# Both output projections as seven quadrant products, with weight sums formed in DRAM

## The chip, the cores and the metric

The kernel runs on one core of a Trainium2 chip. The metric is the device time of one execution in microseconds (us), lower is better; the median of several runs is compared. The core has a matrix engine (TensorE, PE in the profile, with its weight loads shown apart as PEld), a vector engine (DVE), a scalar engine (ACT), a general engine (GpSimd, POOL) and SyncE (SP), whose queue issues nearly all DMA transfers here. The engines run side by side, each through its own instructions in a fixed order, and wait for one another by semaphores. The program on each engine is fixed when the kernel is built.

## What is computed

A decoder trunk of two layers over 512 tokens of width 1024. Each layer normalises x, projects it with one matrix into the inputs of four head groups, mixes, gates, concatenates the four outputs to y (512 x 1024) and adds one output projection to the residual stream:

```python
def hybrid_layer(x, positions, ..., w_out):
    h = rmsnorm(x, norm_g)
    p = h @ w_in
    ...
    y = jnp.concatenate([o_a * jax.nn.silu(g_a), o_b * jax.nn.silu(g_b),
                         o_c * jax.nn.silu(g_c), o_d * jax.nn.silu(g_d)], axis=-1)
    return y @ w_out

for l in range(DEPTH):
    x = x + hybrid_layer(x, ...)
```

All of it is float32. The kernel keeps that precision on PE by splitting every operand into a high and a low part (type fp32r) and making three products of them: high x high, high x low, low x high.

## The kernel before

The 1024 rows of k are cut into eight tiles of 128 (`KT`), the tokens into four (`NT`). A "unit" is 512 KB of weights: `load_units` brings it from DRAM into one of two raw buffers (`rawS`), `split_units` makes its high part on ACT (or DVE) and its low part on DVE, in two halves, into one of six slots (`wS`). Loads and splits run ahead of their use as far as free buffers let them.

`Order` and `Chain` are a planner. Each piece of work is a generator which carries an estimated time (`ch.t`); the planner resumes the generators by due time and priority and so writes the instructions of each engine in the order in which it expects them to become ready. Nothing is reordered on the chip: an instruction whose operand is late holds up all that stand behind it on its engine, DMA issues on the queues of SP and POOL included.

A layer runs in this order on PE: `c` (low-rank inputs of the latent attention), the two token-major units `sq` and `kv`, sixteen feature units (`ga` to `gc1`), with the attention heads woven between them, and then the output projection, `o` in the profile. `put_y` splits a finished row block of y into `yTh` and `yTl` (`yD` for the last two). The last to be finished is block 5, after the last feature product `gc1`.

The output projection runs two column halves of 512, four token tiles each; each (half, token tile) is eight k tiles with three matmuls of 512 columns, accumulated in one PSUM bank (`part`, `YORDER`). `out_chain` adds the bank to the residual row tile `L.x[t]` on DVE; in layer 0 it also sums squares on ACT, sends the finished row tile to DRAM (`x1d`) and starts `pre_norm` of layer 1: two small POOL operations for the factor, a scaling `h` on DVE, eight transposes `hT` on PE, and a split into `hTh` and `hTl`, which `cq` of layer 1 reads. The last token tile of layer 1 is done in two pieces of 256 columns (`TAIL`), so that the end is short.

POOL also builds the rotary tables at the start and turns rotary pairs of Q and K (`rope`), which the attention heads wait for.

Of the kernel before, what the change touches and what calls it, by code (L numbers as in the profile page):

```python
# [196 lines left out]
def hybrid_trunk(ctx: ExitStack, tc: tile.TileContext, x, positions, norm_g, w_c, w_f, w_t, w_o, mla_q_norm_g,  # L197
# [52 lines left out]
    def mm3(ch, n, dst, sh, sl, mh, ml, first, last):  # L250
        c = cost(n)
        yield from ch.pe(c, PE.matmul, dst, sh, mh, start=first, stop=False)
        yield from ch.pe(c, PE.matmul, dst, sh, ml, start=False, stop=False)
        yield from ch.pe(c, PE.matmul, dst, sl, mh, start=False, stop=last)

    def dma(ch, nbytes, dst, src):

# [32 lines left out]
    def add_unit(*a):  # L290
        u = Unit(*a)
        units[u.name] = u
        u.idx = len(order)
        order.append(u)

    FEATS = ["ga0", "ga1", "ch0", "ch1", "cb0", "cb1", "cc0", "cc1", "gb0", "gb1", "su0", "su1",
             "gc0", "gc1", "gd0", "gd1"]
    TOKS = {"sq": ("sv", "mq"), "kv": ("mk", "mv")}
# [2 lines left out]
    for l in range(DEPTH):  # L301
        for kq in range(4):
            add_unit(w_c[l, kq], 2, 416, f"c{kq}_{l}")
        add_unit(mla_w_uq[l], 2, 384, f"uq_{l}")
        add_unit(mla_w_ukv[l], 1, 512, f"ukv_{l}")
        for n in SEQ:
            if n in TOKS:
                for kq in range(4):
                    add_unit(w_t[l, list(TOKS).index(n), kq], 2, 512, f"{n}{kq}_{l}")
            else:  # L310
                add_unit(w_f[l, FEATS.index(n)], 8, P, f"{n}_{l}")
        for half in range(2):
            for kq in WORDER:
                add_unit(w_o[l, half, kq], 2, 512, f"wo{half}{kq}_{l}")

    def load_units():
        for u in order:
            ch = Chain(o)
            u.raw_slots = rawS
            if u.name in ("c2_0", "c3_0"):  # L320
# [60 lines left out]
    hTh = big.tile([P, KT, S], F32R, name="hTh")  # L381
    hTl = big.tile([P, KT, S], F32R, name="hTl")
    yTh = big.tile([P, KT - 2, S], F32R, name="yTh")
    yTl = big.tile([P, KT - 2, S], F32R, name="yTl")

# [125 lines left out]
    for l in range(DEPTH):  # L511
        L = Layer()
        L.l = l
        L.ng_ev = Event()
        L.hT = [[Event(), Event()] for _ in range(NT)]
        L.xss = [cst.tile([P, 4], F32, name=f"xss{t}_{l}") for t in range(NT)]
        L.qd = [Event() for _ in range(NT)]
        L.kd = [Event() for _ in range(NT)]
        L.stat = [Event() for _ in range(NT)]
        L.Vt, L.Mt, L.gates, L.gate_ev, L.MD = {}, {}, {}, {}, {}  # L520
        L.md_ev = {n: [Event() for _ in range(NT)] for n in ("mq", "mk", "mv")}
        L.vt_ev = [Event() for _ in range(NT)]
# [4 lines left out]
        L.mix_ev, L.mla_ev, L.QK_ev = Event(), Event(), Event()  # L527
        L.x = [None] * NT
# [15 lines left out]
    def pre_norm(L, t, xx, t0, release):  # L544
        ch = Chain(o, t0)
        s1 = L.xss[t]
        yield from ch.pool(G.tensor_scalar, s1[:, 2:3], s1[:, 0:1], s1[:, 1:2], EPS, op0=ALU.add, op1=ALU.add)
        yield from pow_rstd(ch, s1[:, 3:4], s1[:, 2:3], 1)
        yield from ch.wait(L.ng_ev)
        h = yield from hS.get(ch, f"h{t}_{L.l}")  # L550
        hput = shared(hS, 2)
        tps = []
        for c in range(2):
            sl = slice(c * 512, (c + 1) * 512)
            yield from ch.dve(V.scalar_tensor_tensor, h[:, sl], in0=xx[:, sl], scalar=s1[:, 3:4], in1=L.ng[c],
                              op0=ALU.mult, op1=ALU.mult)
            tps.append(ch.t)
        release(ch)
        if t == NT - 1:
            for _ in range(2):  # L560
                (t2S if L.l else sS).put(ch)

        def half(c):
            c2 = Chain(o, tps[c])
            tp = yield from trS.get(c2, f"hT{t}_{c}_{L.l}")
            for k in range(4):
                kt = c * 4 + k
                yield from c2.pe(109.0, PE.transpose, tp[:, k * P:(k + 1) * P], h[:, kt * P:(kt + 1) * P], ident)
            hput(c2)
            yield from split2(c2, hTh[:, c * 4:c * 4 + 4, t * P:(t + 1) * P],  # L570
                              hTl[:, c * 4:c * 4 + 4, t * P:(t + 1) * P], tp.rearrange("p (k n) -> p k n", k=4))
            trS.put(c2)
            o.set(L.hT[t][c], c2.t)
        for c in range(2):
            o.spawn(half(c))

    def rope(ch, x1, x2, cb, sb, nh, nd, name):
        tab = yield from rbS.get(ch, f"rb{name}")
# [77 lines left out]
    def q_chain(L, t, q_ps, t0):  # L656
        ch = Chain(o, t0)
        l = L.l
        if t == 0:
# [121 lines left out]
    def y_tiles(L, kt):  # L781
        hi, lo = (yTh, yTl) if kt < 6 else L.yD
        return hi[:, kt % 6, :], lo[:, kt % 6, :]

    def put_y(ch, L, kt, yv):
        if kt == 6:
            L.yD = []
            for i in range(2):
                L.yD.append((yield from ydS.get(ch, f"yD{i}_{L.l}", [P, 2, S], F32R)))
        yield from split2(ch, *y_tiles(L, kt), yv)  # L790
        o.set(L.y[kt], ch.t)

    def su_chain(j):
        def f(L, a, t0):
# [237 lines left out]
    def mla_heads(L):  # L1032
# [37 lines left out]

        yield from heads(L, "a", L.Vt, prep, qk)
        o.set(L.mla_ev, o.now)

    def moba_heads(L):
        ch0 = Chain(o)
# [69 lines left out]
    def out_chain(L, half, t, a, t0, c0=0, c1=512):  # L1145
# [10 lines left out]
        elif half == 1:  # L1156
# [5 lines left out]
                v4S.put(c2)  # L1162
            o.spawn(pre_norm(layers[l + 1], t, L.x[t], ch.t, release))


    def main():
        m = Chain(o)

        def tok(L, n, width, t, dst, us):

            for k in range(KT):
                if n == "c" and k % 4 == 0:
                    yield from m.wait(L.hT[t][k // 4])
                if t == 0 and k % 2 == 0:
                    us.append((yield from unit(m, f"{n}{k // 2}_{L.l}")))
                wh, wlo = us[k // 2]
                yield from mm3(m, width, dst, hTh[:, k, t * P:(t + 1) * P], hTl[:, k, t * P:(t + 1) * P],
                               wh[:, k % 2, :], wlo[:, k % 2, :], k == 0, k == KT - 1)
                if t == NT - 1 and k % 2 == 1:
                    done_unit(f"{n}{k // 2}_{L.l}")  # L1180
                yield o.now

        def done_unit(name):
            if units[name].slots is not eS:
                units[name].slots.put(m)

        early_put(m)
        for L in layers:
# [19 lines left out]
            for n in SEQ:  # L1208
# [10 lines left out]
                else:  # L1219
                    a = yield from accS.get(m, f"{n}_{l}")  # L1220
                    wh, wlo = yield from unit(m, f"{n}_{l}")
                    for k in range(KT):
                        yield from mm3(m, S, a, wh[:, k, :], wlo[:, k, :], hTh[:, k, :], hTl[:, k, :],
                                       k == 0, k == KT - 1)
# [4 lines left out]
            for half in range(2):  # L1229
                us = {}  # L1230

                def part(t, a, i0, i1, c0=0, c1=512):
# [42 lines left out]
    def start():  # L1275
# [52 lines left out]
        hS.put(ch)  # L1328
        o.set(L0.ng_ev, ch.t)

    o.spawn(start())
    o.run()

# [49 lines left out]
```

## Time and profile before

| what | value |
|---|---|
| median of 3 runs | 509.28 us (508.9 to 509.54) |
| the profiled execution | 508.65 us, its span 506.8 us |
| DMA, all transfers | 51.57 MB, mean 102 GB/s |
| output projection, layer 0 / layer 1 | 214.4 to about 260.6 us / 459.5 to 503.4 us |

Times inside the profile count from the start of the span; what lies between the span and the execution's time is start and end of the program. A line of the groups view names the source line (nearly all are one helper's line, so tiles are the better name), engine, operation, written and read tiles, shapes and count, then the busy time, the mean of one, and the idle time of the engine just before these, with what ended it. In the timeline the columns are start, length, engine, line, operation; "x3" is three instructions run into one another; a time in brackets is idle time before. Lengths of neighbours overlap, since engines are pipelined: the step from one start to the next is what an instruction costs in a row of its kind.

### The profile page before, as it was taken

What the parts mean: (1) busy time and instruction counts of PE and PEld (TensorE: products, weight loads), DVE (VectorE), ACT (ScalarE), POOL (GpSimd) and SP (SyncE); (2) the same over time, 40 slices, a digit from 0 to 9 for tenths busy, and PEclk for the clock granted to TensorE, in tenths of its full rate; (3) what the DMA queues carried; (4) which work ended last, traced back from release to release, by engine and by line L of the source; (5) the groups of instructions that cost most, each with busy time, mean ns of one, the idle gap of its engine ahead of it and who ended that gap; (6) DMA issues with size and microseconds to landing.
All of it is one profiled execution on the core that took longest, in us unless ns stands there. A gap on an engine that the chain in (4) does not pass through costs nothing.

```text
span 506.8 us, 7665 instructions
## 1 busy us (share of the span) xinstructions
PE 498.1 (98%) x2508; PEld 423.3 (84%) x2508; DVE 349.3 (69%) x917; ACT 296.5 (58%) x891; POOL 139.2 (27%) x321
## 2 busy tenths in 40 slices
PE   6999999999999999999999999999999999999997
PEld 4898888888888888888889988888888888888886
DVE  4877975468799887635576988777868887635311
ACT  5698764567687775424247894677766777432100
POOL 6867875452000000000121488513330000000000
PEclk9999999999999999999999999999999999999999
DMA  8533415112114123464443242140142121624111
GB/s 273 165 123 114 125 43 166 41 43 66 60 43 166 52 74 109 142 175 117 143 155 126 83 125 71 55 124 2 42 167 82 43 83 49 201 84 164 66 54 50
DMA packets 20618, 51.57 MB, mean 102 GB/s; under 512 B 5985, under 2 KB 7265, under 8 KB 20578
## 3 DMA queue, kind: packets, MB, share of 16 engines
q1 hardware_dynamic: 20546, 51.08, 31.1%
q8 instruction: 20, 0.33, 0.3%
q0 software_dynamic: 32, 0.00, 0.1%
q14 instruction: 20, 0.16, 0.1%
HBM read 46.87 MB, written 4.19 MB: 101 GB/s over the span
## 4 chain that ended last, share of the span: by engine, by line
PE 90%; POOL 4%; DVE 2%; DMA 2%; ACT 1%; issue 1%; POOLq 0%; DVEq 0%
PE o L184 17%; PE kv L184 10%; PE cq L184 6%; PE sq L184 5%; PE cc L184 4%; PE gb L184 4%; PE cb L184 4%; PE gd L184 4%; PE gc L184 4%; PE ch L184 4%; PE su L184 4%; PE sa L184 3%; PE ga L184 3%; PE oa L184 2%; PE od L184 2%; PE sd L184 2%
## 5 line engine op out<-in xcount | busy, mean ns | idle before, releaser
L158 DVE TENSOR_TENSOR xr<-o,xr 128x512 f32<-128x512 f32 (+1 forms) x17 | 11.2, 658 | 42.0 <-PE o L184 42.0
L184 PE MATMUL o<-whi_wo,yTl 128*128 128x512 f32 (+1 forms) x102 | 38.4, 377 | 0.0
L184 PE MATMUL o<-wlo_wo,yTh 128*128 128x512 f32 (+1 forms) x102 | 38.4, 377 | 0.0
L184 PE MATMUL o<-whi_wo,yTh 128*128 128x512 f32 (+1 forms) x102 | 38.4, 376 | 0.0
L158 ACT ACTIVATE whi_wo<-raw_wo 128x512 fp32r<-128x512 f32 x31 | 18.3, 624 | 21.7 <-PE o L184 13.6
L158 ACT ACTIVATE pa<-pa,mna 128x256 f32<-128x256 f32 (+3 forms) x44 | 23.4, 539 | 5.2 <-DVE mna L158 5.1
L184 PE MATMUL kv<-whi_kv,hTh 128*128 128x512 f32 x64 | 26.0, 406 | 0.0
L184 PE MATMUL o<-whi_wo,yD 128*128 128x512 f32 (+1 forms) x68 | 25.7, 381 | 0.0
L158 ACT ACTIVATE pd<-pd,mnd 128x256 f32<-128x256 f32 (+3 forms) x46 | 24.5, 546 | 2.0 <-DVE mnd L158 1.5
L158 ACT ACTIVATE pha<-pTa 128x512 fp32r<-128x512 f32 (+3 forms) x32 | 13.9, 434 | 20.1 <-PE pTa L184 19.9
L184 PE MATMUL kv<-whi_kv,hTl 128*128 128x512 f32 x64 | 25.1, 392 | 0.0
L184 PE MATMUL kv<-wlo_kv,hTh 128*128 128x512 f32 x64 | 24.9, 390 | 0.0
L158 ACT ACTIVATE phd<-pTd 128x512 fp32r<-128x512 f32 (+3 forms) x32 | 13.9, 435 | 18.4 <-PE pTd L184 18.3
L184 PE MATMUL cq<-whi_c,hTh 128*128 128x416 f32 x64 | 24.3, 380 | 0.0
L184 PE MATMUL cq<-whi_c,hTl 128*128 128x416 f32 x64 | 23.3, 365 | 0.0
L184 PE MATMUL cq<-wlo_c,hTh 128*128 128x416 f32 x64 | 23.0, 360 | 0.0
L158 DVE TENSOR_TENSOR wlo_wo<-raw_wo,whi_wo 128x512 fp32r<-128x512 f32 x32 | 21.0, 687 | 2.4 <-ACT whi_wo L158 2.0
L184 PEld LDWEIGHTS o<-wlo_wo,yTh 128*128 128x128 f32 x102 | 19.2, 188 | 3.6
L184 PEld LDWEIGHTS o<-whi_wo,yTh 128*128 128x128 f32 x102 | 19.2, 188 | 3.6
L184 PEld LDWEIGHTS o<-whi_wo,yTl 128*128 128x128 f32 x102 | 19.2, 188 | 3.5
L158 DVE CUSTOM_DVE_ANT_0 pa<-sa,maskb 128x512 f32<-128x512 f32 (+3 forms) x32 | 15.0, 485 | 8.7 <-PE pTa L184 4.6
L158 DVE TENSOR_TENSOR pld<-pTd,phd 128x512 fp32r<-128x512 f32 (+3 forms) x32 | 15.5, 486 | 4.9 <-ACT phd L158 4.8
(328 smaller groups left out, 1712.8 us busy)
## 6 DMA issues: line engine op xcount, KB each, us to landing
raw_wo<-in_w_o_dram SPq DMA_DIRECT2D x16, 512.0 KB, 3.9
raw_sq<-in_w_t_dram SPq DMA_DIRECT2D x8, 512.0 KB, 3.5
raw_kv<-in_w_t_dram SPq DMA_DIRECT2D x8, 512.0 KB, 3.5
raw_c<-in_w_c_dram SPq DMA_DIRECT2D x8, 416.0 KB, 4.2
raw_ga<-in_w_f_dram SPq DMA_DIRECT2D x4, 512.0 KB, 3.6
raw_su<-in_w_f_dram SPq DMA_DIRECT2D x4, 512.0 KB, 3.5
raw_gc<-in_w_f_dram SPq DMA_DIRECT2D x4, 512.0 KB, 3.6
raw_ch<-in_w_f_dram SPq DMA_DIRECT2D x4, 512.0 KB, 3.4
```

What stands on the lines that cost most here:

```text
L158: f(*a, **k)
L184: f(*a, **k)
```

## The change

With the tokens in two halves and k and the output columns in two halves, y @ w_out is a product of two 2 x 2 block matrices. Instead of its eight block products the changed kernel forms seven (Winograd's scheme), each 256 tokens x 512 of k x 512 columns, in the order `ZPROD`: b11, t3, b21, t4, t2, t1, b22. Products named b take a quadrant of the weights as it is; t1 to t4 take a sum: t1 = b11 + b12, t3 = b12 + b22, t2 = t1 + b22, t4 = t2 + b21.

- *The weight sums* are formed in DRAM (`t_sums`). A plain copy DRAM to DRAM (SP queue, 512 KB, 16 rows of 32 KB) puts the first addend in place, then an accumulating transfer (POOL queue, 512 KB as 512 pieces of 1 KB) adds the second. There are eight copies and eight sums a layer; t2 is copied from the finished t1, t4 from the finished t2, so those copies wait on SP's queue for the sums. Layer 0's begin during its `sq` stage, layer 1's when layer 0's latent attention is through.
- *The weight units* of the projection are fourteen a layer instead of eight; the second of each product lands in the two buffers of Q and K (`tkS`).
- *y's sums*: in `put_y` the blocks 0 to 3 first get tokens 256-511 replaced by (tokens 0-255 minus them). Each block of y is written to DRAM as float32 (`ysc`). `s_chain` reads a pair of blocks back, forms three sums of 256 columns on DVE and splits them into `sumh`/`suml`. These take the memory of `hTh`/`hTl`, which now are allocated per layer; the splits of layer 1's `hT` wait until the last product of layer 0 has read the sums (`h_done`).
- *The banks*: each product has two banks of 128 tokens. b21 accumulates on b11, t4 on t3; a third pair of banks starts as minus b11 (an ACT copy with scale -1) and t2, t1 and b22 accumulate on it. `z_out` adds or subtracts a bank to a residual half after each product: twelve operations of 512 columns a layer instead of eight, one more at the end of layer 1.
- *The order of tokens*: row tiles 2, 3, 0, 1 are finished in this order, and `cq` of layer 1 takes them so.

```diff
+SEVEN = (0, 1)
+K0, K1, KK = (2, 3, 0, 1), (4, 5, 6, 7), (0, 2, 3, 1)
+ZPROD = ("b11", "t3", "b21", "t4", "t2", "t1", "b22")
...
+    def t_sums(l):
+        for steps in ((("t1", "b11", "b12"), ("t3", "b12", "b22")), (("t2", "t1", "b22"),), (("t4", "t2", "b21"),)):
+            for n, a, _ in steps:
+                for j in range(2):
+                    o.clk["D"] = max(o.clk["D"], o.now) + 1500.0
+                    nc.sync.dma_start(z_src(l, n, j), z_src(l, a, j))
+                    yield o.now + 4000.0
+            yield o.now + 4000.0
+            for n, _, b in steps:
+                for j in range(2):
+                    o.clk["G"] = max(o.clk["G"], o.now) + 1000.0
+                    nc.gpsimd.dma_start(z_src(l, n, j), quad(l, b, j), accum_op=ALU.add, max_dma_last_dim=1024)
+                    yield o.now + 4000.0
+            yield o.now + 8000.0
...
+            if L.l:
+                yield from c2.wait(layers[L.l - 1].h_done)
+            if c not in L.h:
+                L.h[c] = [big.tile([P, 4, S], F32R, tag=f"h{x}{c}", name=f"hT{x}{c}_{L.l}") for x in "hl"]
...
+        if L.seven and kt in K0:
+            yield from ch.dve(V.tensor_tensor, yv[:, 256:512], yv[:, 0:256], yv[:, 256:512], op=ALU.subtract)
+        t0 = ch.t
         yield from split2(ch, *y_tiles(L, kt), yv)
         o.set(L.y[kt], ch.t)
+        if L.seven:
+            nc.sync.dma_start(ysc[L.l][kt], yv)
...
+    def s_chain(L, kk):
...
+        yield from ch.dve(V.tensor_tensor, b[:, 256:512], b[:, 256:512], a[:, 256:512], op=ALU.add)
+        yield from ch.dve(V.tensor_tensor, b[:, 0:256], b[:, 0:256], b[:, 256:512], op=ALU.subtract)
+        c2 = Chain(o, ch.t)
+        yield from ch.dve(V.tensor_tensor, a[:, 0:256], a[:, 0:256], b[:, 256:512], op=ALU.subtract)
+        yield from split2(c2, *(z[:, kk, :] for z in L.sums[0]), b)
...
+        yield from split2(ch, *(z[:, kk, :] for z in L.sums[1]), a[:, 0:256])
...
+            def prod(n, i, a, first, c0=0, c1=512):
+                for x, kk in enumerate(KK):
+                    if (n, kk // 2) not in us:
+                        us[n, kk // 2] = yield from unit(m, f"{n}{kk // 2}_{l}")
+                    wh, wlo = us[n, kk // 2]
+                    yh, yl, ev = left(n, kk, i)
+                    yield from m.wait(ev)
+                    yield from mm3(m, c1 - c0, a[:, c0:c1], yh, yl, wh[:, kk % 2, c0:c1], wlo[:, kk % 2, c0:c1],
+                                   first and x == 0, x == 3, not first)
...
+            for n in ZPROD:
+                for i in range(2):
...
+                    yield from prod(n, i, a, n in ("b11", "t3"))
+                    if n == "b11":
+                        y = bank[f"y{i}"] = yield from sS.get(m, f"oy{i}_{l}")
+                        o.spawn(minus(i, a, y, o.now + PELAT, ev))
+                    else:
+                        o.spawn(z_out(L, n, i, a, o.now + PELAT, ev,
+                                      slot[b].put if n in ("b21", "t4", "b22") else None))
...
-            for t in range(NT):
+            for t in L.torder:
```

More of the change, by code (lines that the diff above doesn't have):

```diff
@@ L248, in split2, with mm3 @@
         yield from ch.dve(V.tensor_tensor, lo, src, hi.bitcast(F32), op=ALU.subtract)
-    def mm3(ch, n, dst, sh, sl, mh, ml, first, last):
+    def mm3(ch, n, dst, sh, sl, mh, ml, first, last, go_on=False):
         c = cost(n)
-        yield from ch.pe(c, PE.matmul, dst, sh, mh, start=first, stop=False)
-        yield from ch.pe(c, PE.matmul, dst, sh, ml, start=False, stop=False)
-        yield from ch.pe(c, PE.matmul, dst, sl, mh, start=False, stop=last)
+        k = dict(skip_group_check=True) if go_on else {}
+        yield from ch.pe(c, PE.matmul, dst, sh, mh, start=first, stop=False, **k)
+        yield from ch.pe(c, PE.matmul, dst, sh, ml, start=False, stop=False, **k)
+        yield from ch.pe(c, PE.matmul, dst, sl, mh, start=False, stop=last, **k)
     def dma(ch, nbytes, dst, src):
@@ L311, in hybrid_trunk @@
                 add_unit(w_f[l, FEATS.index(n)], 8, P, f"{n}_{l}")
+        if l in SEVEN:
+            for n in ZPROD:
+                for j in range(2):
+                    add_unit(z_src(l, n, j), 2, 512, f"{n}{j}_{l}")
+            continue
         for half in range(2):
@@ L319, in load_units @@
             u.raw_slots = rawS
-            if u.name in ("c2_0", "c3_0"):
+            if u.name in ("c2_0", "c3_0") or u.name[:-3] in ZPROD and u.name[-3] == "1":
                 u.raw_slots = tkS
@@ L527, in hybrid_trunk @@
         L.mix_ev, L.mla_ev, L.QK_ev = Event(), Event(), Event()
+        L.seven = l in SEVEN
+        L.hT_free, L.h_done, L.h = Event(), Event(), {}
+        L.s = {n: [Event() for _ in range(4)] for n in ("t2", "t1", "b22")}
+        L.left, L.s4 = {}, [Event(), Event()]
+        L.QK_taken = False
+        L.torder = (2, 3, 0, 1) if l and layers[l - 1].seven else (0, 1, 2, 3)
         L.x = [None] * NT
@@ L569, in half @@
             hput(c2)
-            yield from split2(c2, hTh[:, c * 4:c * 4 + 4, t * P:(t + 1) * P],
-                              hTl[:, c * 4:c * 4 + 4, t * P:(t + 1) * P], tp.rearrange("p (k n) -> p k n", k=4))
+            if L.l:
+                yield from c2.wait(layers[L.l - 1].h_done)
+            if c not in L.h:
+                L.h[c] = [big.tile([P, 4, S], F32R, tag=f"h{x}{c}", name=f"hT{x}{c}_{L.l}") for x in "hl"]
+            yield from split2(c2, *(z[:, :, t * P:(t + 1) * P] for z in L.h[c]), tp.rearrange("p (k n) -> p k n", k=4))
             trS.put(c2)
@@ L658, in q_chain @@
         l = L.l
-        if t == 0:
+        if not L.QK_taken:
+            L.QK_taken = True
             L.Q = yield from tkS.get(ch, f"Q{l}", 96)
@@ L1072, in mla_heads @@
         o.set(L.mla_ev, o.now)
+        if L.l == 0:
+            for l in SEVEN:
+                if l:
+                    o.spawn(t_sums(l), None, 4)
     def moba_heads(L):
@@ L1163, in out_chain, with row_done, release, z_out @@
             o.spawn(pre_norm(layers[l + 1], t, L.x[t], ch.t, release))
+    def row_done(L, t, half, t0, junk_):
+        l = L.l
+        cols = slice(half * 512, half * 512 + 512)
+        if l == DEPTH - 1:
+            nc.sync.dma_start(out[0, t * P:(t + 1) * P, cols], L.x[t][:, cols])
+            return
+        ch = Chain(o, t0)
+        yield from square_half(ch, layers[l + 1], t, half, junk_, L.x[t])
+        L.left[t] = L.left.get(t, 2) - 1
+        if L.left[t]:
+            return
+        nc.sync.dma_start(x1d[t * P:(t + 1) * P, :], L.x[t])
+        tend = ch.t + 4000.0
+        def release(c):
+            v4S.put(Chain(o, max(c.t, tend)))
+        o.spawn(pre_norm(layers[l + 1], t, L.x[t], ch.t, release))
+    def z_out(L, n, i, a, t0, ev, put, c0=0, c1=512):
+        ch = Chain(o, t0)
+        for t, half, op, done in {"t3": ((2 + i, 1, ALU.subtract, False),), "b21": ((i, 0, ALU.add, True),),
+                                  "t4": ((2 + i, 0, ALU.add, False),), "t2": ((2 + i, 0, ALU.subtract, True),),
+                                  "t1": ((2 + i, 1, ALU.add, True),), "u": ((i, 1, ALU.add, False),),
+                                  "b22": ((i, 1, ALU.add, True),)}[n]:
+            yield from ch.wait(L.xr[t])
+            xx = L.x[t][:, half * 512 + c0:half * 512 + c1]
+            k = dict(in0=xx, in1=a[:, c0:c1]) if op == ALU.subtract else dict(in0=a[:, c0:c1], in1=xx)
+            yield from ch.dve(V.tensor_tensor, out=xx, op=op, **k)
+            if done and (c0, c1) != (0, 512):
+                nc.sync.dma_start(out[0, t * P:(t + 1) * P, half * 512 + c0:half * 512 + c1], xx)
+            elif done:
+                if n == "t2":
+                    yield from ch.wait(L.s4[i])
+                if n in ("t1", "t2") and L.l < DEPTH - 1:
+                    junk_ = yield from trS.get(ch, f"jk{t}{half}")
+                else:
+                    junk_ = a
+                yield from row_done(L, t, half, ch.t, junk_)
+                if n in ("t1", "t2") and L.l < DEPTH - 1:
+                    trS.put(ch)
+        o.set(ev, ch.t)
+        if n == "t4":
+            o.set(L.s4[i], ch.t)
+        if put:
+            put(ch)
     def main():
@@ L1173, in tok @@
                     yield from m.wait(L.hT[t][k // 4])
-                if t == 0 and k % 2 == 0:
+                if len(us) == k // 2:
                     us.append((yield from unit(m, f"{n}{k // 2}_{L.l}")))
                 wh, wlo = us[k // 2]
-                yield from mm3(m, width, dst, hTh[:, k, t * P:(t + 1) * P], hTl[:, k, t * P:(t + 1) * P],
+                hh, hl = hk(L, k)
+                yield from mm3(m, width, dst, hh[:, t * P:(t + 1) * P], hl[:, t * P:(t + 1) * P],
                                wh[:, k % 2, :], wlo[:, k % 2, :], k == 0, k == KT - 1)
-                if t == NT - 1 and k % 2 == 1:
+                if t == (L.torder[-1] if n == "c" else NT - 1) and k % 2 == 1:
                     done_unit(f"{n}{k // 2}_{L.l}")
@@ L1222, in main @@
                     for k in range(KT):
-                        yield from mm3(m, S, a, wh[:, k, :], wlo[:, k, :], hTh[:, k, :], hTl[:, k, :],
+                        yield from mm3(m, S, a, wh[:, k, :], wlo[:, k, :], *hk(L, k),
                                        k == 0, k == KT - 1)
@@ L1227, in main @@
                     o.spawn(fns[n](L, a, o.now + PELAT))
-            for half in range(2):
+            if L.seven:
+                yield from seven(L)
+            else:
+                o.set(L.h_done, o.now)
+            for half in range(0 if L.seven else 2):
                 us = {}
```

83 lines of the change are left out of this document (80 added, 3 removed).

## The prediction

> **What bounds the kernel now.** I read the page first: the busy shares and the chain that ended last.
>
> ```profile
> PE 498.1 (98%) x2508; PEld 423.3 (84%) x2508; DVE 349.3 (69%) x917; ACT 296.5 (58%) x891; POOL 139.2 (27%) x321
> ...
> PE 90%; POOL 4%; DVE 2%; DMA 2%; ACT 1%; issue 1%; POOLq 0%; DVEq 0%
> PE o L184 17%; PE kv L184 10%; PE cq L184 6%; PE sq L184 5%; PE cc L184 4%; PE gb L184 4%; PE cb L184 4%; PE gd L184 4%; PE gc L184 4%; PE ch L184 4%; PE su L184 4%; PE sa L184 3%; PE ga L184 3%; PE oa L184 2%; PE od L184 2%; PE sd L184 2%
> ```
>
> PE is busy from end to end, the chain is PE for 90%, and the output projection `o` is its largest part. Then the chain in order of time, for the price of a matmul and for the two stages that change:
>
> ```profile
> 138.16 0.70 PE gd L184 x3
> ...
> 214.39 31.96 PE o L184 x141
> 246.35 0.87 PE hT L184 x8
> 247.22 5.47 PE o L184 x24
> ...
> 448.15 5.44 PE su L184 x24
> ...
> 459.50 43.84 PE o L184 x216
> ```
>
> 24 matmuls of 512 columns take 5.44 us, 0.2267 each. Layer 1's projection is 168 of 512 and 48 of 256 columns, worth 192 of 512: 192 x 0.2267 = 43.5 against 43.84 seen. So that stage never waits for operands. What the other engines do in these two stages:
>
> ```profile
> 214.40:260.60 46.20, 46.20 (x217) 38.45 (x217) 22.70 (x36) 15.80 (x34) 3.87 (x8) 1.00 0.47 144
> ...
> 459.50:503.40 43.90, 43.83 (x216) 37.08 (x215) 12.46 (x20) 5.74 (x10) 0.00 (x0) 1.00 0.25 91
> ```
>
> These are rows of the windows view: stretch, its length, then busy time and count of PE, PEld, DVE, ACT, POOL, the granted clock (1.00) and DMA's share. DVE is half idle in layer 0's stage, more in layer 1's. The room that the change wants to spend is there.
>
> **The change part by part.**
>
> *PE.* Seven products of 24 matmuls are 168 a layer, where there were 192: 48 fewer in all, the end's cut into 256 columns kept. 48 x 0.2267 = **-10.88 us**. All lie in a stage that PE alone sets, so all of it counts unless a wait moves in.
>
> *DVE in the projection stage.* The rows:
>
> ```profile
> L158 DVE TENSOR_TENSOR wlo_wo<-raw_wo,whi_wo 128x512 fp32r<-128x512 f32 x32 | 21.0, 687 | 2.4 <-ACT whi_wo L158 2.0
> L158 DVE TENSOR_TENSOR xr<-o,xr 128x512 f32<-128x512 f32 x15 | 10.3, 690 | 37.4 <-PE o L184 37.4
> L158 DVE TENSOR_TENSOR xr<-o,xr 128x256 f32<-128x256 f32 x2 | 0.8, 425 | 4.6 <-PE o L184 4.6
> L158 ACT ACTIVATE whi_wo<-raw_wo 128x512 fp32r<-128x512 f32 x31 | 18.3, 624 | 21.7 <-PE o L184 13.6
> ...
> 211.67 1.89 DVE L158 TENSOR_TENSOR wlo_wo<-raw_wo,whi_wo 128x512 fp32r<-128x512 f32 x3
> 217.24 0.69 DVE L158 TENSOR_TENSOR yTl<-u,yTh 128x512 fp32r<-128x512 f32 x1
> ```
>
> In the built order, eighteen low halves of weight units stand in layer 0's stage against eight before: +10 x 0.687 = 6.9. The sums of y are four times three operations of 256 columns, one split of 512 and one of 256: 4 x (4 x 0.425 + 0.687) = 9.5. Four more residual updates: 4 x 0.69 = 2.8. With the 22.70 of before that is 41.9 us of lengths; but three in a row take 1.89, a step of 0.60 for a length of 0.69, so DVE needs 41.9 x 0.60/0.69 = 36.4 us in a stage of 38.1 (plus some transposes). Full, but not over. Layer 1 has no next layer to prepare: 12.46 + 19.2 = 31.7, 27.5 by the step. The order matters too: block 5 of y is split at 217.24, 2.9 us after the stage starts, and the sums stand behind it; they are wanted only by the fifth product, 4 x 5.44 = 21.8 us in. The tightest place I find is b211's second half: it stands behind an update that waits for t3's first bank (5.44 + 2.72 = 8.2 us in), then needs some five operations to 10.7, and PE wants it at 10.9 + 0.7 + 0.7 = 12.3. I take **+0.5** for the stages; bounds 0 and 4.4 (all 41.9 + the rest at full length, 42.5 against 38.1, in layer 0). ACT gains ten high halves, eight splits of sums (half of them half as wide) and two negated copies, at most 20 x 0.624 = 12.5 us on 15.80, and stays under.
>
> *The layer boundary.* Before, `hT` of token tile 3 was split beside the last matmuls:
>
> ```profile
> 259.77 0.40 PE L184 MATMUL o<-whi_wo,yD 128*128 128x512 f32 x1
> 260.01 0.60 PE L184 MATMUL hT<-ident,h 128*128 128x128 f32 x4
> 260.36 0.43 PE L184 MATMUL cq<-whi_c,hTh 128*128 128x416 f32 x1
> 260.64 0.35 PE L184 MATMUL cq<-wlo_c,hTh 128*128 128x416 f32 x1
> ...
> 259.52 0.60 ACT L158 ACTIVATE hTh<-hT 128x512 fp32r<-128x512 f32 x1 [2.72 <-PE hT L184]
> 260.15 0.69 DVE L158 TENSOR_TENSOR hTl<-hT,hTh 128x512 fp32r<-128x512 f32 x1 [0.81 <-ACT hTh L158]
> ```
>
> `cq` started at once. Now `hTh` may be written only when the last matmul of b22 is through: that one's start + 0.40, then ACT 0.60, then DVE 0.69 until the third `cq` matmul, 1.7 us. PE covers of it its own 0.23, four transposes 0.44 and two `cq` matmuls at 0.19: 1.05. So **+0.7**; nothing if a tile's memory came free earlier, 2.5 if DVE is behind by three operations (the scaling of the next token tile and two low parts stand beside it). The other sixteen transposes that now fall behind the boundary are moved, not added.
>
> *POOL's issues.* POOL's one transfer of before also has 512 pieces (of 4 bytes):
>
> ```profile
> 2.21 0.99 POOL L395 DMA_DIRECT2D posi<-in_positions_dram  x1
> 79.55 0.61 POOL L158 TENSOR_TENSOR rbk<-krt,sinT 128x64 f32<-128x64 f32 x2 [4.82 <-DVE Q L158]
> ...
> 92.38 0.60 POOL L158 TENSOR_TENSOR Q<-Q,rbq 128x64 f32<-128x64 f32 x2
> ...
> 96.54 0.44 PE t0a L184 x4
> ...
> posi<-in_positions_dram POOLq DMA_DIRECT2D x1, 2.0 KB, 5.0
> ```
>
> It held POOL for 0.99. Four of layer 0's eight sums stand among the rotary work of 65 to 80 us, four x 0.99 = 4.0; POOL waits 4.82 for DVE there, and what it makes is ready at 93.0, 3.5 before PE transposes it. Cost **0**; without that cover 4.0. The upper bound is an issue that holds POOL until the data has landed, 5.0 us: 4 x 5.0 - 4.82 - 3.5 = 11.7 less the 4.0 that the build's order allows for: 7.7. The other twelve stand where POOL has only a few memsets, or before the `pre_norm` of layer 1.
>
> The Trainium skill speaks against this place: "SBUF — State Buffer", section "SBUF: two separate sides", says that the descriptors of a GpSimd-issued transfer are written by GpSimd's own cores, and that VectorE's double-rate copies lock them out (about 620 ns became 3100). By that factor an issue would hold POOL 5 us, and the time would be that of the second rival; by the row, 1. No run here shows yet an issue beside such copies.
>
> *SP's queue and the DRAM traffic.*
>
> ```profile
> DMA packets 20618, 51.57 MB, mean 102 GB/s; under 512 B 5985, under 2 KB 7265, under 8 KB 20578
> ...
> raw_wo<-in_w_o_dram SPq DMA_DIRECT2D x16, 512.0 KB, 3.9
> ...
> x1d<-xr SPq DMA_DIRECT2D x4, 512.0 KB, 2.6
> ...
> 97.36 8.25 SPq L259 DMA_DIRECT2D raw_gd<-in_w_f_dram  x2
> ...
> 212.38 7.89 SPq L259 DMA_DIRECT2D raw_wo<-in_w_o_dram  x4
> ```
>
> Layer 0's copy of t1 into t2 waits for the sum of t1 and stands on SP ahead of `raw_gd`, which was issued at 97.36 and used by PE only at 138.16. So the wait may last 30 us before a split is late. A sum of 512 KB is not in the trace: at best one pass, 3.9; at most read, read and write after one another, 3.9 + 3.9 + 2.6 = 10.4. The nearest thing is several transfers overlapping, so I take 5 to 6: cost **0**. Copies (8 MB), sums (8), y out and back (8) and twelve more units (6) add some 30 MB to 51.57, where DMA's share is 0.47 in the busier projection stage: 0.
>
> *Subtraction in blocks 0 to 3.* Eight operations of 0.425 on DVE, under attention that PE leads: **+0.2** (0 to 3.4). The end is the same cut of 256 columns: 0.
>
> Sum: 508.65 - 10.88 + 0.5 + 0.7 + 0.2 = 499.2 for the profiled execution, 9.5 less. The median of the runs stands 0.63 above that execution, so **499.8 us**.
>
> **The rivals.**
>
> 1. *The weight sums are slow (slower).* Fourteen of the sixteen must be through before layer 0 loads its second half of t2: SP holds that load behind t4's copies of layer 1, which wait for t2's sums. PE wants it 22 us after 214.39, so issued by about 231. From 65 to 231 us that is 166/14 = 11.9 us a sum if they follow one another. Below it nothing happens; at 13 us the load is 14 x 13 - 166 = 16 late and PE stands: 499.8 + 16 = **516**. For it: the bound of 10.4 is not far, and pieces of 1 KB are small. Against: transfers overlapped well in the trace.
> 2. *POOL held at issue*: 499.8 + 7.7 = **507.5**. For it: the 5.0 us to landing; against: the 0.99.
> 3. *DVE becomes the bound in layer 0's projection*: 42.5 for 38.1: 499.8 - 0.5 + 4.4 = **503.7**. For it: 36.4 of 38.1 leaves no slack after a late load; against: units are split up to three products ahead.
> 4. *No gain*: rivals 2 and 3 together, or t4's copy waiting at a worse place: about 509.
>
> **How the numbers follow.** Chances: forecast 0.66 (498.4, which is only the 10.88, to 503), DVE bound 0.08, POOL held 0.10, no gain 0.04, slow sums 0.12. A change under 0.2% (1.0 us) can't be told from none in this kernel. Faster by more: 0.66 + 0.08 + 0.10 = 0.84, of which I leave 0.01 to slower; same 0.04; slower 0.13 with that. The range from 498.3 to 507 holds the forecast, the DVE case and part of POOL's; below lies nothing but noise, above the slow sums and the no-gain case, under 2 in 10 in all.
>
> **What would show each step.** Right: 168 records a layer in the projection at a step of 0.2267, layer 0's stage near 39.5 us with its transposes, layer 1's near 38.5; a gap of under 1 us before the third `cq` matmul; POOL's issues near 1 us each and `t0a` not later than about 98; SP's waits for sums short, `raw_gd` landed long before 138. Wrong: PE idle before t2 or t4 with a DMA as releaser (slow sums); PE idle at `t0a` or `sa` after POOL (rival 2); PE idle inside the seven products behind `wlo` or `suml` (rival 3). If the sum of idle time on PE before these exceeds 10 us, the forecast fails in its sign.

## The result and the profile after

| kernel | median | runs | ratio to before, 95% interval |
|---|---|---|---|
| before | 508.84 us (508.03 to 509.77) | 10 | |
| changed | 511.15 us (508.86 to 513.26) | 10 | 1.0041 (1.0023 to 1.0058) |

The change makes the kernel 0.4% slower; 499.8 us was predicted. The profiled execution took 510.08 us, its span 508.3. First its page: the busy shares, the granted clock in 40 slices, and the chain that ended last.

```profile
PE 490.7 (97%) x2448; PEld 414.6 (82%) x2448; DVE 386.4 (76%) x1005; ACT 317.9 (63%) x936; POOL 154.7 (30%) x328
...
PEclk9999999999999999999799999999999999999999
...
DMA packets 35915, 83.03 MB, mean 163 GB/s; under 512 B 7201, under 2 KB 16673, under 8 KB 35618
...
PE 77%; DVE 7%; ACT 5%; DMA 4%; POOL 2%; issue 2%; SPq 1%; DVEq 0%; ACTq 0%
```

PE is still busy for 97%, but it carries the chain for 77% only, where it was 90%. The one "7" in the clock row marks the place: the slice from 241 to 254 us, near the end of layer 0's projection. Here is the chain there, in order of time (start, length, what).

```profile
237.78 0.38 SPq L264
...
238.25 9.23 DMA raw_b<-in_w_o_dram
...
247.59 0.64 ACT whi_b L161
...
248.86 0.69 DVE xr L161
249.68 7.31 PE oy L187 x24
...
264.02 0.69 DVE hTl L161
264.85 0.63 PE hT L187 x4
265.48 1.13 PE cq L187 x6
...
466.41 5.44 PE oz L187 x24
471.85 5.44 PE ox L187 x24
477.29 5.44 PE oz L187 x24
482.73 5.44 PE ox L187 x24
488.17 13.60 PE oy L187 x60
501.77 2.88 PE ot L187 x24
```

Layer 1's projection is what was forecast: 38.2 us from 466.41 to 504.65, where it was 43.84, and no gap in it. Layer 0's is not. PE waits for a transfer of weights of b22 that took 9.23 us. PE's timeline gives the waits in brackets. The second matmul of t1 starts 0.56 us after the first, where the step of a row is 0.23; the third line is the first matmul of b22:

```profile
249.68 0.77 PE L187 MATMUL oy<-whi_t,sumh 128*128 128x512 f32 x1 [6.71 <-DVE xr L161]
250.24 0.63 PE L187 MATMUL oy<-wlo_t,sumh 128*128 128x512 f32 x1
...
256.81 0.39 PE L187 MATMUL oy<-whi_b,sumh 128*128 128x512 f32 x1
...
264.85 0.63 PE L187 MATMUL hT<-ident,h 128*128 128x128 f32 x4 [1.49 <-DVE hTl L161]
```

The windows view of the same stage (busy time of PE, PEld, DVE, ACT, POOL, then granted clock, DMA share, GB/s):

```profile
222.00:228.00 6.00, 6.00 (x28) 4.99 (x27) 5.78 (x14) 5.56 (x13) 0.00 (x0) 1.00 0.93 331
228.00:234.00 6.00, 6.00 (x29) 4.95 (x28) 6.00 (x13) 2.31 (x6) 0.00 (x0) 1.00 0.79 244
234.00:240.00 6.00, 6.00 (x28) 4.99 (x27) 3.53 (x7) 2.06 (x6) 4.43 (x4) 1.00 0.63 128
240.00:246.00 6.00, 2.97 (x14) 2.12 (x12) 1.89 (x3) 1.68 (x3) 0.00 (x0) 1.00 1.07 312
246.00:252.00 6.00, 2.32 (x6) 1.89 (x7) 4.47 (x7) 4.20 (x11) 0.00 (x0) 0.52 1.14 290
252.00:258.00 6.00, 6.00 (x26) 4.92 (x25) 3.37 (x6) 2.70 (x8) 0.90 (x2) 0.91 0.57 183
```

From the first `oz` (215.61) to the first `cq` of layer 1 (265.24) the stage takes 49.6 us. The wait before t1 is 6.71. From t1's first matmul to b22's are 7.13 us instead of 5.44 (+1.69; the 7.31 of the chain counts to the end of the last matmul): by the clock column (0.52 of 6 us, then 0.91) 5.8 us of the row from 246 to 252 and 1.1 us of the next were at half clock, so the clock fell at about 246.2, during the wait, and came back at about 253. The wait at the boundary is 1.49. Together 9.9, and 49.6 - 9.9 = 39.7, close to the 39.5 forecast for the stage without them. So the stage has its 24 fewer matmuls and lost ten microseconds to three things.

Why the weights were late: between 234 and 240 the DMA engines are not full (0.63, 128 GB/s), from 240 on they are. SP's queue says what it did in between:

```profile
226.07 1.10 SPq L322 DMA_DIRECT2D t<-t  x2
227.47 0.33 SPq L264 DMA_DIRECT2D raw_t<-t  x1
227.85 0.42 SPq L525 DMA_DIRECT2D cg_b<-in_mla_q_norm_g_dram  x1
...
236.27 0.94 SPq L264 DMA_DIRECT2D ng<-in_norm_g_dram  x2
237.31 0.85 SPq L264 DMA_DIRECT2D raw_t<-t  x2
238.25 1.32 SPq L264 DMA_DIRECT2D raw_b<-in_w_o_dram  x2
```

From 227.85 to 237.2 SP issues the small loads of layer 1's parameters and norm gain. The kernel before had them at 220 to 228 us, in the projection too, but behind the last of its eight weight units; now there are fourteen to bring in. Behind them stand the weights of t1 and b22, and when these start, they meet the two sums of layer 1's t4, issued by POOL at 236.7, which land in 14.3 us (the median of the two). Two causes are possible, then: the *queue* and the *traffic*. The experiments were to tell them apart. The chain also shows a third thing: t1's first matmul waits for t2's update of its bank, and that update stands on DVE behind the split of b22.

### The profile page after: what moved, and what is told of

It is laid out like the page before. It is cut to its first block, busy times and chain, and to the rows that moved or that the text cites. A ratio compares the mean times of both kernels' runs of the same rounds, so it can differ in the third digit from the quotient of the medians.

```text
span 508.3 us, 7837 instructions
## 1 busy us (share of the span) xinstructions
PE 490.7 (97%) x2448; PEld 414.6 (82%) x2448; DVE 386.4 (76%) x1005; ACT 317.9 (63%) x936; POOL 154.7 (30%) x328
## 4 chain that ended last, share of the span: by engine, by line
PE 77%; DVE 7%; ACT 5%; DMA 4%; POOL 2%; issue 2%; SPq 1%; DVEq 0%; ACTq 0%
PE kv L187 10%; PE cq L187 6%; PE cb L187 4%; PE ch L187 4%; PE gd L187 4%; PE cc L187 4%; PE gb L187 4%; PE su L187 4%; PE oy L187 4%; PE gc L187 4%; PE sa L187 3%; PE ox L187 2%; PE oz L187 2%; ACT junk L161 2%; PE od L187 2%; PE sd L187 2%
## 5 line engine op out<-in xcount | busy, mean ns | idle before, releaser
L328 POOL DMA_DIRECT2D t<-in_w_o_dram x16 | 16.9, 1085 | 38.6 <-DMA t<-t 35.1
L161 ACT ACTIVATE pd<-pd,mnd 128x256 f32<-128x256 f32 (+3 forms) x50 | 26.7, 547 | 2.4 <-DVE mnd L161 2.1
L161 DVE TENSOR_TENSOR wlo_t<-raw_t,whi_t 128x512 fp32r<-128x512 f32 x32 | 21.0, 682 | 6.7 <-ACT whi_t L161 6.7
L161 ACT ACTIVATE whi_t<-raw_t 128x512 fp32r<-128x512 f32 x32 | 18.5, 620 | 11.7 <-DMA raw_t<-t 11.7
L187 PE MATMUL oy<-whi_t,sumh 128*128 128x512 f32 x32 | 13.3, 417 | 6.7 <-DVE xr L161 6.7
L161 DVE TENSOR_TENSOR pla<-pTa,pha 128x512 fp32r<-128x512 f32 (+3 forms) x32 | 15.2, 482 | 5.8 <-ACT pha L161 5.7
L187 PE MATMUL sq<-yTh,hTh 128*128 128x512 f32 x48 | 18.9, 393 | 0.0
L187 PE MATMUL sq<-yTh,hTl 128*128 128x512 f32 x48 | 18.7, 390 | 0.0
L187 PE MATMUL sq<-yTl,hTh 128*128 128x512 f32 x48 | 18.7, 390 | 0.0
L161 DVE TENSOR_TENSOR wlo_b<-raw_b,whi_b 128x512 fp32r<-128x512 f32 x24 | 15.9, 684 | 1.5 <-ACT whi_b L161 1.3
L161 DVE CUSTOM_DVE_ANT_0 pd<-sd,maskb 128x256 f32<-128x256 f32 (+3 forms) x32 | 15.0, 484 | 2.2 <-PE pTd L187 2.2
```

Of the source, the lines that this page charges most:

```text
L161: f(*a, **k)
L187: f(*a, **k)
L328: nc.gpsimd.dma_start(z_src(l, n, j), quad(l, b, j), accum_op=ALU.add, max_dma_last_dim=1024)
```

## The experiments

All are edits of the changed kernel. First, one change at a time.

**Parameter loads behind t1.**

```diff
                 if n == "t3" and l + 1 < DEPTH:
                     o.spawn(load_norm_gain(layers[l + 1]))
+                if n == "t1" and l + 1 < DEPTH:
                     load_params(layers[l + 1])
```

> Edit: the eleven kinds of small parameter loads of layer 1 are issued after product t1 instead of after t3; only the norm gain stays after t3. Theory Q (queue): the wait of 6.71 us before t1 at 249.68 us comes from SP issuing these loads (227.85 to 236.2) ahead of the weights of t1 and b22. Then those loads go out some 4 to 8 us earlier, t1's wait falls below 2 us, the clock does not fall behind it, and the time is 511.1 - 6.7 - 1.9 = about 502.5 (502 to 505). Theory T (traffic): DMA is full from 240 to 252 us (share 1.07 and 1.14) with the sums of layer 1's t4 and the weight loads; then earlier issue only lengthens the landing, t1 waits 5 us or more and the time stays at 509 to 511.

508.17 us (505.19 to 511.61), ratio 0.9985 (0.996 to 1.0009). The wait before t1 fell from 6.71 to 0.77 us, the projection from 49.6 to 42.1 us, as the queue theory said. The time did not follow: `cq` to `sq` of layer 1 took 32.5 us instead of 26.7, of which 4.0 are two waits of PE (3.26 and 0.77) and most of the rest is a clock at half from 266.5 to 269.9 us. The run with both edits, below, shows the same with fewer things in it.

**Layer 1's sums later.**

```diff
-        if L.l == 0:
-            for l in SEVEN:
-                if l:
-                    o.spawn(t_sums(l), None, 4)
...
+                    if n == "sq" and l in SEVEN and l:
+                        o.spawn(t_sums(l), None, 4)
```

> Edit: the forming of layer 1's weight sums starts in layer 1 after its unit sq, instead of at the end of layer 0's latent attention; parameter loads stay where they are. Theory Q: t1's weights are issued at about 236 (the two t4 copies of 1.4 us leave the queue), the wait before t1 stays at 4 us or more: 508 to 511. Theory T: without layer 1's copies and sums in layer 0's projection the load of b22's first half lands in 4.6 us instead of 9.2, t1's wait falls to 2 us or less: 502 to 505. Rival to both (the sums cost wherever they lie): layer 1's attention loses what layer 0's projection gains, 509 to 512.

505.92 us (503.51 to 507.84), ratio 0.9939 (0.9915 to 0.9963). The wait fell to 3.39 us, and t1 took 5.74 us. The load of b22 landed in 7.95 us, not 4.6, with the parameter loads still around it. Layer 1's attention did not pay for the sums: `sq` to the projection took 174.3 us in both kernels. So traffic had a part in the wait, and a larger part in the time than the queue had.

**Both.**

> Edits of the two other runs together. If queue and traffic each cost a part, this is the fastest of the three: no wait above 1 us before t1, clock at 1.00 throughout, layer 0's projection (first product to layer 1's third cq matmul) 41 to 42 us instead of 49.7, time 501 to 503. Theory Q alone: as the run with the parameters moved. Theory T alone: as the run with the sums moved.

506.12 us (504.45 to 507.81), ratio 0.9943 (0.9926 to 0.996). No wait before t1, clock at 1.00, and the stage at 41.1 us; but not 501 to 503. The chain of this run tells where the gain went:

```profile
255.38 0.61 DVE xr L161
...
256.08 4.59 DMA raw_c<-in_w_c_dram
...
262.96 0.69 DVE hTl L161
263.70 1.11 PE hT L187 x4
264.81 1.04 PE cq L187 x3
```

The parameter loads, now issued from 248.26 to 254.8, stand ahead of the last quarter of `cq`'s weights (`raw_c`, 256.08), and on DVE `hTl` stands behind the split of that quarter. `cq` to `sq` took 30.9 us instead of 26.7: a wait of 2.46 us before the transposes at 263.70, and a clock at half from 263.3 to 266.7, are nearly all of it. The queue's cost was moved, not removed.

**The two layers apart.**

```diff
-SEVEN = (0, 1)
+SEVEN = (1,)
```

> Edit: SEVEN = (1,): layer 0 keeps its eight products, no sums of y and no sums of weights for it; layer 1 has seven. My reading: layer 1's projection is shorter by 24 matmuls, 5.4 us, and nothing else is lost: 508.8 - 5.5 = about 503.4 (502.5 to 504.5). Rival: forming layer 1's sums beside layer 0's old projection delays that one as well (its loads landing in 8 us or more): 506 to 510.

503.48 us (503.29 to 504.56), ratio 0.9891 (0.9874 to 0.9907): -5.5, as worked out. Layer 1's projection starts 199.1 us after the first `cq` (199.0 before), with layer 1's sums formed beside layer 0's old projection, which still took 46.1 us.

```diff
-SEVEN = (0, 1)
+SEVEN = (0,)
```

> Edit: SEVEN = (0,): layer 0 alone has seven products, layer 1 its eight; no weight sums for layer 1. My reading: layer 1's seven gave 5.5 us by themselves, so what the whole change lost lies in layer 0: its body about 1 us longer (sums of y, subtraction), its projection still with a wait before t1 behind the parameter loads (3 us or so, as where layer 1's sums were put off), layer 1's attention 1 us longer. About 511 (509.5 to 512.5). Rival (layer 0's seven cost nothing once layer 1's sums are away): 504 to 506.

513.04 us (512.57 to 513.53), ratio 1.0076 (1.0058 to 1.0094). Layer 0 alone costs +4.0. With -5.5 from layer 1 that would make -1.5; the changed kernel has +2.3. The 3.8 between arise only where layer 1's sums meet layer 0's seven products; the wait before t1, 6.71 with them and 3.59 without, is 3.1 of it. Beside eight products the sums cost nothing that shows.

This run and the one with layer 1's sums late differ in one small thing with a large result. These are t1's product in the chains of the two, layer 0 alone first:

```profile
247.42 7.31 PE oy L187 x24
```

```profile
247.12 5.74 PE oy L187 x24
```

The waits before them were 3.59 and 3.39 us. After the first the clock fell, after the second it did not.

**No weight sums at all.**

```diff
     def t_sums(l):
+        return
...
-                    add_unit(z_src(l, n, j), 2, 512, f"{n}{j}_{l}")
+                    add_unit(quad(l, {"t1": "b12", ...}.get(n, n), j), 2, 512, f"{n}{j}_{l}")
```

> Edit: as the changed kernel, but no weight sum is formed in either layer: each product named t loads one plain quadrant in its place (left out: 16 copies and 16 accumulating transfers; the output is not the reference's). Parameter loads stay after t3. Theory Q and T both in part: time like the run with layer 1's sums put off, 505 to 507, with a wait of 2 to 4 us left before t1. Theory Q alone: 508 or more. Theory T alone: no wait, 502 to 503.5.

This leaves out the 16 copies and 16 accumulating transfers; each t product reads a plain quadrant, so the output is not y @ w_out. 508.23 us (507.09 to 510.86), ratio 0.999 (0.9974 to 1.0007): a miss, above 505 to 507. The wait was 3.61 us, within 2 to 4, but t1 took 7.33: the clock fell. So more than 3 us of the wait are there without any sum; the next run shows that the parameter loads make them. Attention also had another wait of 1.15 us (at 182 us, DVE), in an order that the planner made anew.

**The parameter loads where SP is free.** PE comes to layer 0's unit su1 at about 200 us. The loads go there; the sums of layer 1 stay late.

```diff
             for n in SEQ:
+                if n == "su1" and l + 1 < DEPTH:
+                    load_params(layers[l + 1])
...
                     o.spawn(load_norm_gain(layers[l + 1]))
-                    load_params(layers[l + 1])
```

> Edits: layer 1's sums after its sq, as before, and layer 1's parameter loads when PE comes to layer 0's unit su1, where SP has nothing queued for 6 us; the norm gain stays after t3. Behind t1 these loads held up the last piece of cq's weights instead (cq to sq 30.9 us instead of 25.6). Theory Q+T: no wait before t1 (under 1 us) and cq to sq 26 to 27 us: 501 to 503. Rival (any place on SP costs the same, since the loads before the seven products are then late): PE waits at b11 or t3, 505 to 507.

501.84 us (500.99 to 502.47), ratio 0.9858 (0.9842 to 0.9875). This beats both kernels. On SP the loads of t1's weights now go out at 230.42 and those of b22 at 233.50, where they went at 237.31 and 238.25. Its windows, columns as above:

```profile
222.00:228.00 6.00, 6.00 (x28) 4.90 (x27) 5.76 (x13) 5.20 (x12) 0.00 (x0) 1.00 0.67 240
228.00:234.00 6.00, 6.00 (x27) 4.88 (x27) 6.00 (x13) 2.34 (x5) 0.00 (x0) 1.00 0.84 259
234.00:240.00 6.00, 6.00 (x28) 4.98 (x27) 6.00 (x12) 5.58 (x13) 0.00 (x0) 1.00 0.69 266
240.00:246.00 6.00, 6.00 (x28) 4.97 (x27) 5.00 (x9) 3.38 (x8) 0.00 (x0) 1.00 0.56 171
246.00:252.00 6.00, 6.00 (x30) 4.97 (x29) 4.51 (x9) 3.32 (x8) 2.66 (x4) 1.00 0.77 252
```

PE is busy throughout and the clock is full, with DVE without a pause from 228 to 240.

**The same move without the other.** Only the parameter loads go to su1:

> Edit: only the parameter loads are moved to the unit su1; layer 1's sums stay beside layer 0's projection. Theory Q: no wait above 1 us before t1, clock at 1.00, layer 0's projection 41 to 42.5 us, cq to sq 26 to 27.5 us, time 502 to 504. Theory T: with the sums' traffic beside them the weights of t1 and b22 still land late, wait 2 to 5 us, 505 to 508.

508.31 us (503.84 to 509.82), ratio 0.9966 (0.9939 to 0.9992). The profiled execution (506.25 us) had 1.23 us before b21 and 2.85 before t1. With SP free the loads of b22 went out 3 us earlier (235.34) and landed late all the same. Here are the two kinds of transfer that meet, between 226 and 252 us: in this run,

```profile
raw_t<-t SPq DMA_DIRECT2D x3, 512.0 KB, 8.8
...
t<-in_w_o_dram POOLq DMA_DIRECT2D x2, 512.0 KB, 15.0
raw_b<-in_w_o_dram SPq DMA_DIRECT2D x2, 512.0 KB, 9.9
```

and with layer 1's sums late as well:

```profile
raw_t<-t SPq DMA_DIRECT2D x3, 512.0 KB, 5.3
raw_b<-in_w_o_dram SPq DMA_DIRECT2D x2, 512.0 KB, 5.0
```

The medians of the four kernels make a square:

| | sums of layer 1 beside layer 0's projection | later |
|---|---|---|
| parameter loads after t3 | 511.15 | 505.92 |
| parameter loads at su1 | 508.31 | 501.84 |

Moving the loads is worth 2.8 or 4.1, moving the sums 5.2 or 6.5, both 9.3. Neither theory alone stands; each cause is enough to make PE wait.

**DVE's order.** The planner is told that three loads land later, so that t2's two updates stand ahead of b22's split (and one ahead of t1's second).

```diff
             dma(ch, P * u.a * u.b * 4, u.raw[:, :u.a * u.b], u.src)
+            ch.t += {"t11_0": 2000.0, "b220_0": 4000.0, "b221_0": 4000.0}.get(u.name, 0.0)
             o.set(u.loaded, ch.t)
```

> Edit: the planner is told that the loads of t1's second half and of b22 (layer 0) land 2 and 4 us later than it assumes, so on DVE t2's two residual updates stand ahead of those splits; queue and traffic are left as in the changed kernel. Theory O (the order on DVE turns late weights into the wait: t1's first matmul waits for t2's update of its bank, which stands behind the split of b22, not for its own weights): those were there from about 245 us, so the wait falls from 6.7 to 2 to 3 us, in pieces, t1 runs nearer to its 5.44 us, and the time is 504.5 to 507.5. Rival (t1's own weights are what is late, the order is nothing): the wait stays at 5 us or more, 509.5 to 512.

510.19 us (508.48 to 511.35), ratio 1.002 (1.0007 to 1.0033). The wait is now for t1's own weights:

```profile
236.97 9.15 DMA raw_t<-t
...
246.20 1.16 ACT whi_t L161 x2
...
247.42 11.28 PE oy L187 x36
```

It is 5.02 us instead of 6.71, but the clock fell all the same and PE worked under it for longer: half from 246.7 to 253.5 us, and t1 8.40 us from its first matmul to b22's instead of 7.13. The boundary's wait grew to 2.64. The theory of DVE's order falls but for the 1.7 us of the wait, which came back in these two places: t1's weights were late too.

**The boundary.** On top of the run with both moved: the upper half of `hT` may be written when t1 is through, and `cq` takes k tiles 4 to 7 first.

```diff
-                yield from c2.wait(layers[L.l - 1].h_done)
+                yield from c2.wait(layers[L.l - 1].h_done[c])
...
+                if n == "t1":
+                    o.set(L.h_done[1], o.now)
...
-            for k in range(KT):
+            for x, k in enumerate((4, 5, 6, 7, 0, 1, 2, 3) if n == "c" and L.l else range(KT)):
```

> The edits of the run with the parameters at su1, and: the upper half of hT (k tiles 4 to 7), whose memory held only the sums of t1, is written as soon as t1 is through, not when b22 is; cq of layer 1 takes k tiles 4 to 7 first. Theory: the wait of 1.49 us for hTl at the layer boundary and some of the 1.0 us in cq go: 1 to 2 us less than the run with the parameters at su1, 499.5 to 502. Rival: the wait only moves to k tile 0, as the lower half is bound by the same DVE order: within 0.5 us of it.

503.11 us (500.99 to 504.93), ratio 0.9871 (0.9843 to 0.9898). The wait fell from 1.50 to 0.81 us, and the stage is 0.5 us shorter in the trace; but from `sq` of layer 1 to its projection took 176.8 us instead of 174.3, of which 0.9 show as longer waits behind `vnh` and `vnl` at 315 us; the clock then fell to half from 316.4 to 319.8, which costs the other 1.7. The gain at the boundary came back as a longer wait later and its half clock. The time is not told apart from the kernel without the edit.

**Layer 0's sums later.** On top of the run with both moved, too: they begin at the planner's 88 us instead of 36, behind POOL's rotary work.

> Edits of the run with the parameters at su1 and layer 1's sums late, and: layer 0's sums begin about 50 us later, behind the rotary work of POOL instead of among it. Theory (POOL's issues of 1.1 us among the rotary pairs cost up to 1.2 us before t0a in some executions): no wait at t0a, layer 0 from sq to its projection 175.1 to 175.6 us instead of 175.8 to 177.1, time 0.3 to 1 us less, 500.8 to 501.6. Rival (the later sums push t4 behind its load): PE waits before t2 or t4, 503 or more.

504.75 us (502.89 to 507.85), ratio 0.993 (0.9892 to 0.9967): a miss. No wait at `t0a`, but new ones: 1.14 us at 183 us, and 0.38 and 1.25 before matmuls of b21, behind splits which stand on DVE among the sums of y. Not before t2 or t4, as the rival had it. Where the sums stood was better.

## Why the prediction was wrong

The step that failed is "SP's queue and the DRAM traffic", which was priced at 0. In its place the square above shows 9.3 us: 2.8 to 4.1 for where the parameter loads stand on SP, 5.2 to 6.5 for where layer 1's sums run, the falls of the clock behind them included.

- *What it looked at.* It asked what the new copies on SP could hold up, found `raw_gd` with 30 us to spare, and was right there. It did not ask the reverse, what stands on SP ahead of the new loads. The parameter loads were in the trace of before at 220 to 228 us; eight units left room for them, fourteen did not, and they and the norm gain held the queue for 9.4 us.
- *"DMA's share is 0.47 in the busier projection stage: 0."* That was the share of the kernel before. Y's read back, six more units, and layer 1's copies and sums, which fall in this very stage, take it to 0.57 to 1.14 in the windows above, and loads that land in some 5 us take 9. The Trainium skill, page "DMA: Bandwidth & Descriptors", section "Issuing engines are not separate DMA queues", says that transfers run on the same 16 DMA engines whoever issues them. The landings of 9.9 us beside POOL's sums and 5.0 without agree.
- *"Units are split up to three products ahead"* (against the third rival) holds for the first products only. In the run of the changed kernel b22's last low half is made after t1 has begun.
- *The clock* was in no term. The wait of 6.71 us cost 1.69 more.

The other steps:

- *PE, -10.88*: right in layer 1 (38.2 us against 38.5, -5.5 measured by layer 1 alone), and right in layer 0 once the waits are taken off (39.7 against 39.5). With both causes moved, the kernel gains 7 us of the 9.5.
- *DVE, +0.5* (0 to 4.4): within its bounds. No wait in the seven products of the run with both moved, with DVE at 6.00 of 6.00 us in two windows. The third rival's mechanism shows at 1.6 us in the run with layer 0's sums late.
- *Boundary, +0.7* (0 to 2.5): mis-sized, PE waits 1.49. The four transposes were to cover part of it; in the trace they stand behind it themselves, since they wait for `hTl` (264.85 above).
- *POOL's issues, 0*: the size was right: 16 issues in 16.9 us, 1.01 to 1.47 each. The estimate of 5 us that was worked out from the Trainium skill ("SBUF — State Buffer", "SBUF: two separate sides") did not come true; its rule speaks of copies on DVE, and in the trace of the changed kernel no copy ran there beside any of the 16, so it is not tested here. But the cover was thinner than thought: `t0a` waits 0.5 to 1.2 us for Q in four of the runs with layer 0's sums in this place (none in the profiled run of the changed kernel). That POOL's issues make Q late there is not shown.
- *Slow sums* (first rival): a sum lands in 8.1 us by the median, inside the bounds of 3.9 to 10.4 and above the 5 to 6 taken; the slowest took 17.8. It did not come true as told, PE standing for t2 or t4. What it had right is that the sums' time matters, as traffic.
- *Subtraction, +0.2*: layer 1's attention is 0.14 us longer where layer 1 alone has seven products. With layer 0's seven it is 0.9 to 1.0 longer in most runs, of which some 0.6 is one wait of PE for `vnh`, absent before; the run with DVE's order lacks the wait and is 0.3 longer. The order of the token tiles differs there; that it is the cause was not tried.
- *No gain* (fourth rival, about 509): the measured time is near, but by luck. Neither POOL's issues nor a bound DVE made it, and the two copies of t4 took 1.1 us of SP.

For the profiled executions: forecast 499.2, measured 510.08, 10.9 apart. The wait is 6.7, the clock 1.7, the boundary 0.8 over its term, layer 0 and layer 1 between `sq` and projection 0.6 and 0.9 over theirs, and 0.7 lies ahead of layer 0's `sq` (which starts between 39.07 and 40.50 us in the runs here, whatever was edited behind it); the 0.5 for DVE was not needed. The sum is 10.9. The prediction's last sentence put the failure at 10 us of idle time on PE: it was 8.2 us of idle and 1.7 for half clock.

## What to carry to other kernels

When a stage gets shorter and needs more loads, list everything on the issuing queue between its first and last load, old entries first; small loads of 0.4 us each can hold up the large ones that PE waits for. Price a transfer by what else moves in that same window of the new kernel, not by the share of the old one. And a stage that saves PE time at the price of more transfers should be tried with its traffic elsewhere: here the same products gave +0.4% or -1.4%, by where 13 small loads and 16 transfers stood in the order.

## What the runs showed of the hardware

- *The clock around a wait.* The rows of three other stages: the run with both edits, the boundary run, and the one with the parameter loads behind t1.

```profile
263.70 1.11 PE L187 MATMUL hT<-ident,h 128*128 128x128 f32 x4 [2.46 <-DVE hTl L161]
...
264.00:268.00 4.00, 4.00 (x18) 3.51 (x17) 4.00 (x7) 2.43 (x5) 0.49 (x1) 0.66 0.23 77
```

```profile
315.17 0.39 PE L187 MATMUL mp<-vnh,wsh 128*128 128x256 f32 x1 [1.28 <-ACT vnh L161]
...
316.00:320.00 4.00, 4.00 (x18) 3.47 (x18) 2.11 (x8) 1.79 (x4) 3.39 (x16) 0.57 1.11 393
```

```profile
266.00:270.00 4.00, 3.23 (x13) 2.93 (x12) 4.00 (x8) 2.20 (x5) 0.00 (x0) 0.57 0.12 46
```

A share of 0.57 in 4 us is 3.4 us at half clock; the changed kernel, with its wait of 6.71, and the run with DVE's order, with 5.02, had twice that, 6.8. The price is half of PE's work in that time: 1.69 us for t1 in the changed kernel, 3.0 in the run with DVE's order. What brings the fall about is not settled here. Before t1, waits of 2.85 and 3.39 us left the clock whole and waits of 3.59, 3.61, 5.02 and 6.71 did not; but in the rows above it fell beside waits of 2.46 and 1.28 us and behind one of 3.26. So the length of a single wait does not decide. The Trainium skill, "TensorE: Matmul & The Clock Gate", section "What's actually happening", says that the clock is halved after at least one idle window of about 3.4 us. The waits before t1 would fit that, the falls beside 2.46 and 1.28 us do not, and the measurement decides.

- *Accumulating transfers from DRAM to DRAM.* 512 KB in 1 KB pieces land in 8.1 us by the median, 15 beside weight loads, and loads beside them take up to twice as long (9.9 and 8.8 us where they take 5.0 and 5.3 without), while POOL is held for 1.1 us only. Layer 1's cost nothing beside layer 0's eight products or in layer 1's attention, and 5.2 to 6.5 us beside the seven.
